# Whole-tile transfers and two wide rooms instead of half-tile transfers and four narrow ones, in a two-branch attention layer on one core

## The chip, the cores and the metric

The kernel runs on one core of a Trainium2 chip. Its engines are TensorE (PE, with its weight load PEld), VectorE (DVE), ScalarE (ACT), GpSimd (POOL) and SyncE (SP), which issues all transfers. The metric is the device time of one execution in microseconds, as the median of several runs. Less is better.

## The reference

One layer of a hybrid encoder is computed for a prompt of 1024 rows and a sample of 32 rows with the same weights. The width is 1024, and there are 8 heads of 64 in branch A and 8 in branch B.

```python
u = rmsnorm(h, g_pre) @ w_in                 # (rows, 4096): qA kA vA gA qB kB vB gB
oA = band_attention(qA, kA, vA, bias)        # 64-row chunks, own and 8 previous ones, softmax
oB = stick_breaking(qB, kB, vB)              # strictly causal, products of sigmoids
y = concat(oA * silu(gA), oB * silu(gB)) @ w_out
h = h + rmsnorm(y, g_post)
h = h + sigmoid(h @ w_ple_gate) * (p @ w_ple)
```

The sample attends to 512 cached rows as well. Outputs are both results, and the keys and values of both branches. Everything is in 32-bit floats.

## The kernel before, in words

**Recording and order.** The kernel isn't written in the order in which it runs. Each call on an engine is recorded as an operation; `Recorder.order` then simulates the engines with a table of costs and gives each operation a due time, and for each engine the operation with the earliest due time that is ready goes next. In the last pass each due time is shifted by ten times a number from two tables at the head of the file: `AHEAD_OF`, by engine and by the first letters of the written tile's name, and `AHEAD_AT`, by stage as well. `Recorder.emit` writes the instructions in the order so found. On the chip each engine takes its own list in order, and the engines wait for each other by semaphores. All recorded instructions carry the line of one helper, L793, so groups are told apart by the names of tiles.

**Stages.** Stage 0 loads and normalises x, turns it (hnh, hnl), and multiplies the first three column tiles; the per-layer product of the first four row tiles (`Ple(True)`, tiles `pleo`) fills TensorE meanwhile. Stages 1 to 8 weave attention of one head pair (tiles S, be, wTh, wTl, PV) with the projection by the next column tiles (`mm_kA` and so on). Stage 8 ends with the gate columns gA and gB. Stage 9 makes the rest of the per-layer product (`Ple(False)`, row tiles 4 to 8, tiles `ple`), stages 10 and 11 the output projection (`o0P` to `o3P`), stages 12 and 13 the product with w_ple_gate (`g0P` to `g3P`). Every 32-bit factor is split into a high part and a rest in a format that TensorE multiplies fast, and three products are added up.

**Column weights.** A column tile is 1024 x 128 of w_in. `load_w(j)` fetches it ahead of time, as two halves of 512 rows, each into a room of tag `wr` (names `wr_kA` and so on). `ensure(j)` casts each half to its high part (`wh`, on ScalarE; on GpSimd for the first three tiles) and subtracts for the rest (`wl`, on GpSimd). The 32 column tiles so make 64 transfers of 256 KB.

**The tag `wr`.** It has four rooms of 544 columns in 32-bit words on 128 partitions, given out in the order of the program. Besides raw weights it holds, at other times: the sample's split keys (`Kh`, `Kl`), its split cached values and weights (`Vh`, `Vl`, `wh`, `wl`), the late per-layer weights (`wpr`), the late per-layer products on their way to DRAM (`ple`, ten halves of a row tile; two of them take tag `bias` instead), the rows of x for the residual (`Row.load`, two halves per row tile), and product and residual of a gate (`Gate`, `pl` and `hh`). A room is taken again when the last reader of what it held is done; for a stored tile that is when its store has landed.

**Transfers.** SP issues all transfers of the program in the order that the planner found. A transfer whose room or data isn't ready holds up those behind it.

Of the kernel before, what the change touches and what calls it, by code (L numbers as in the profile page):

```python
# [8 lines left out]
F32 = mybir.dt.float32  # L9
F32R = mybir.dt.float32r  # L10
# [3 lines left out]
P = 128  # L14
# [6 lines left out]
KD = 8  # L21
# [6 lines left out]
AHEAD_OF = {  # L28
    ('ACT', 'Kh'): 847, ('ACT', 'L'): -810, ('ACT', 'Qfs'): 1255, ('ACT', 'be'): 110,
    ('ACT', 'gT'): 1212, ('ACT', 'kd'): 494, ('ACT', 'news'): -2591, ('ACT', 'om'): 22,  # L30
    ('ACT', 'stq'): 422, ('ACT', 'stv'): 214, ('ACT', 'v'): 132, ('ACT', 'w'): 1508, ('ACT', 'x'): -702,
    ('DVE', 'Kl'): -1025, ('DVE', 'Vh'): 168, ('DVE', 'Vl'): 157, ('DVE', 'diags'): -1166,
    ('DVE', 'news'): 142, ('DVE', 'o'): -939, ('DVE', 'oT'): -2081, ('DVE', 'sq'): -898,
    ('DVE', 'w'): 331, ('DVE', 'wTl'): -26, ('DVE', 'wl'): -2838, ('PE', 'PV'): -5, ('PE', 'PVl'): 51,
    ('PE', 'S'): -3, ('PE', 'Ss'): 12, ('PE', 'mm'): 7, ('PE', 'o'): -848, ('PE', 'ptws'): -36,
    ('PE', 'ptx'): -23, ('POOL', 'bias'): 574, ('POOL', 'kl'): -1392, ('POOL', 'o'): -923,
# [4 lines left out]
}  # L41
AHEAD_AT = {
# [3 lines left out]
    (1, 'SP', 'swap'): 1043, (2, 'ACT', 'kd'): -796, (2, 'ACT', 'om'): 57, (2, 'ACT', 'stq'): 426,  # L46
    (2, 'ACT', 'stv'): -553, (2, 'ACT', 'wh'): -314, (2, 'DVE', 'vx'): -235, (2, 'PE', 'PVl'): -89,
    (2, 'PE', 'mm'): 25, (2, 'PE', 'ptw'): -3, (2, 'POOL', 'o'): 176, (2, 'SP', 'wr'): -421,
    (3, 'ACT', 'stv'): -962, (3, 'ACT', 'whs'): -1728, (3, 'DVE', 'v'): -2339, (3, 'PE', 'PV'): 36,
# [19 lines left out]
}  # L69
# [729 lines left out]
def stream_step(  # L799
# [75 lines left out]
    def load_w(j):  # L875

        if j >= len(order) or j in raws:
            return
        kind, p = order[j]
        c0 = NAMES.index(kind) * 512 + p * P  # L880
        raws[j] = []
        for kh in range(2):
            raw = wpool.tile([P, 4, P], F32, tag="wr", name=f"wr_{kind}{p}_{kh}", bufs=4)
            dma(raw, w_in[0, kh * 512:(kh + 1) * 512, c0:c0 + P].rearrange("(k p) c -> p k c", p=P))
            raws[j].append(raw)

# [487 lines left out]
    def sample_attention(ab, gi):  # L1374
# [22 lines left out]
        def queries():  # L1397
# [11 lines left out]
            for a in range(2):  # L1409
                hi, lo = (wpool.tile([P, NK], F32R, tag="wr", name=f"K{x}{a}{nm}", bufs=4) for x in "hl")  # L1410
                pt = bx["Kc"][:, a, :]
                nc.vector.transpose(pt, pt)
                nc.scalar.copy(hi[:, 0:PAST], pt)
                nc.vector.tensor_tensor(lo[:, 0:PAST], pt, f(hi[:, 0:PAST]), ALU.subtract)
                new = ksS[:, at_[a], :]
                nc.scalar.copy(hi[:, PAST:NK], new)
                nc.vector.tensor_tensor(lo[:, PAST:NK], new, f(hi[:, PAST:NK]), ALU.subtract)
                Kh.append(hi)
                Kl.append(lo)
# [40 lines left out]
        def weights():  # L1460
            w1 = bx["w1"]
            def place(x, shape):
                return wpool.tile(shape, F32R, tag="wr", name=x + nm, bufs=4)

            def cached(b):
                pair = [place(f"V{x}{b}", [P, 2, 256]) for x in "hl"]
                nc.vector.tensor_copy(pair[0], bx["Vc"][:, b:b + 2, :])
                nc.vector.tensor_tensor(pair[1], bx["Vc"][:, b:b + 2, :], f(pair[0]), ALU.subtract)
                return pair

            old = [cached(0)]
            wh, wl = place("wh", [P, 4, P]), place("wl", [P, 4, P])
            pt = psum("T", f"ptw{nm}")
# [39 lines left out]
    class Ple:  # L1513
# [8 lines left out]
        def load_w(self, k, q):  # L1522
            name = f"wpr{k}_{q}{self.early}"
            if not self.early:
                raw = wpool.tile([P, 512], F32, tag="wr", name=name, bufs=4)
            elif (k, q) == (1, 1):
# [68 lines left out]
        def pieces(self, t, q):  # L1595
            t0, n = rows_of(t)
            hl = self.hl[t // 2]
            if self.early:
                if q == 0:
                    self.outs.append(at.tile([P, D], F32, tag=("kd1", "kl1", "L1", "v21")[t], name=f"pleo{t}"))  # L1600
                out = self.outs[t][:, HALF[q]]
            else:
                out = wpool.tile([P, 512], F32, tag="wr", name=f"ple{t}_{q}", bufs=4) if (t, q) not in ((5, 1), (6, 1)) else at2.tile([P, 512], F32, tag="bias", name=f"ple{t}_{q}", bufs=2)
            acc = psum(("S", "PV")[t - 2] if t > 1 and self.early else "mm" if self.early else "S", f"ple{t}_{q}")
# [9 lines left out]
            else:  # L1614
                nc.scalar.copy(out[0:n], acc[n:2 * n])
                nc.vector.tensor_tensor(out[0:n], acc[0:n], out[0:n], ALU.add)
            if not self.early or q:
                store = dma if not self.early else self.later.append
                args = (ple_dr[t0:t0 + n, HALF[q]], out[0:n]) if not self.early else ((ple_early[:, t, :], self.outs[t]),)
                store(*args)  # L1620

        later, outs = [], []

# [394 lines left out]
    class Row:  # L2018
# [7 lines left out]
        def load(self):  # L2026
            self.x = [wpool.tile([P, 512], F32, tag="wr", name=f"x2_{self.t}_{q}", bufs=4) for q in range(2)]
            for q in range(2):
                dma(self.x[q][0:self.n], x_prompt[0, self.t0:self.t0 + self.n, HALF[q]] if self.t < 8 else x_sample[0][:, HALF[q]])

# [24 lines left out]
    class Gate:  # L2055
        def __init__(self, t, cols, early=False):
# [6 lines left out]
            else:  # L2063
                self.pl = wpool.tile([P, 512], F32, tag="wr", name=f"pl{t}_{cols.start}", bufs=4)
                self.h = wpool.tile([P, 512], F32, tag="wr", name=f"hh{t}_{cols.start}", bufs=4)
            dma(self.pl[0:n], ple_early[32 * t:32 * t + 32].rearrange("q b c -> (q b) c")[:, cols] if t < 4 else ple_dr[self.rows, cols])
# [240 lines left out]
```

## Time and profile before

| | |
|---|---|
| median of 3 runs | 761.14 us (760.43 to 761.95) |
| the profiled execution | 760.99 us, span 759.1 us |
| PE busy | 750.3 us, 99% of the span, 4378 matmuls |
| PEld busy | 689.2 us, 91% |
| DVE, ACT, POOL busy | 606.5, 534.0, 447.5 us |
| transfers' queue | 168.63 MB, 75.9% of 16 engines' span |
| granted clock of TensorE | 1.000 |

The span runs from the first to the last instruction of one profiled execution. A busy PE is one that has a matmul under way, with ends that are modelled; its waits are listed apart. A transfer has an issue on SP and a landing, some microseconds later.

### The profile page before, as it was taken

The numbers are of one execution on the slowest core, as the hardware profiler recorded it, in microseconds if no ns is written. First come the engines' busy times: TensorE is split into PE (matmuls) and PEld (weight loads), VectorE is DVE, ScalarE is ACT, GpSimd is POOL, SyncE is SP. The second block draws the span as 40 slices with busy tenths as digits, with TensorE's granted clock in tenths as the row PEclk, the third lists the DMA queues.
The fourth block names the chain that finished last, engine by engine and source line by source line (L and its number), as shares of the span: only waits on it lengthen the run. The fifth ranks groups of instructions, "written<-read, shape, count | busy, mean of one in ns | idle before, by whom it ended". The sixth has DMA issues, their size and how long they took to land.

```text
span 759.1 us, 13838 instructions
## 1 busy us (share of the span) xinstructions
PE 750.3 (99%) x4378; PEld 689.2 (91%) x4378; DVE 606.5 (80%) x981; ACT 534.0 (70%) x1107; POOL 447.5 (59%) x496
## 2 busy tenths in 40 slices
PE   8999999999999999999999999999999999999997
PEld 7999999999999999999899999999998877888786
DVE  7827867899899998977899788867556788968975
ACT  6647874988687868976879786644348968874561
POOL 5724547773374653657774347877543449696553
PEclk9999999999999999999999999999999999999999
DMA  9645977868777758878878888996789956776864
GB/s 308 201 146 139 249 210 231 240 180 241 205 211 203 208 175 226 219 219 261 231 224 229 206 208 229 264 246 195 214 264 329 288 163 217 277 236 186 303 211 140
DMA packets 198971, 169.52 MB, mean 223 GB/s; under 512 B 66145, under 2 KB 158281, under 8 KB 198898
## 3 DMA queue, kind: packets, MB, share of 16 engines
q1 hardware_dynamic: 198898, 168.63, 75.9%
q8 instruction: 35, 0.57, 0.3%
q14 instruction: 38, 0.31, 0.1%
HBM read 107.82 MB, written 61.01 MB: 222 GB/s over the span
## 4 chain that ended last, share of the span: by engine, by line
PE 94%; DMA 2%; DVE 2%; ACT 1%; SPq 1%; issue 0%; ACTq 0%
PE mm_gB L793 6%; PE mm_kA L793 6%; PE mm_vB L793 6%; PE mm_gA L793 6%; PE mm_qB L793 6%; PE mm_vA L793 6%; PE mm_qA L793 5%; PE mm_kB L793 5%; PE SB L793 4%; PE PVB L793 4%; PE PVA L793 4%; PE SA L793 3%; PE ple L793 3%; PE g1P L793 3%; PE o3P L793 3%; PE o1P L793 3%
## 5 line engine op out<-in xcount | busy, mean ns | idle before, releaser
L793 POOL TENSOR_TENSOR be<-be 128x512 f32<-128x512 f32 (+8 forms) x66 | 86.1, 1313 | 56.5 <-ACT be L793 19.6
L793 DVE TENSOR_TENSOR_SCAN be<-be,unit 128x383 f32<-128x383 f32 (+7 forms) x100 | 93.2, 948 | 17.3 <-ACT be L793 16.2
L793 ACT ACTIVATE be<-SB 128x512 f32<-128x512 f32 (+5 forms) x192 | 83.8, 514 | 17.3 <-PE SB L793 12.6
L793 DVE TENSOR_TENSOR wTl<-be,wTh 128x640 fp32r<-128x640 f32 (+3 forms) x56 | 66.9, 1203 | 5.6 <-ACT wTh L793 5.5
L793 DVE STREAM_TRANSPOSE be<-be 128x640 f32<-128x640 f32 (+3 forms) x64 | 54.4, 849 | 6.7 <-POOL be L793 3.2
L793 ACT ACTIVATE be<-be,statA 128x640 f32<-128x640 f32 (+2 forms) x64 | 44.6, 698 | 15.3 <-DVE statA L793 11.5
L793 ACT CAST wTh<-be 128x640 fp32r<-128x640 f32 (+3 forms) x56 | 42.3, 762 | 1.8 <-DMA be<-swapB 1.6
L793 POOL TENSOR_TENSOR gB<-gB,gB 128x256 f32<-128x256 f32 x32 | 25.5, 820 | 20.2 <-DMA gB<-in_w_ple_gate_dram 20.2
L793 DVE CUSTOM_DVE_ANT_0 be<-SA,biasA 128x320 f32<-128x320 f32 (+2 forms) x64 | 30.0, 478 | 7.6 <-PE SA L793 4.0
L793 POOL TENSOR_TENSOR oB<-oB,oB 128x256 f32<-128x256 f32 x32 | 27.4, 875 | 9.9 <-DMA oB<-in_w_out_dram 9.8
L793 PE MATMUL SB<-kdB,LB 128*128 128x384 f32 (+5 forms) x96 | 33.1, 346 | 0.0
L793 PE MATMUL SB<-kl,LB 128*128 128x384 f32 (+5 forms) x96 | 33.1, 345 | 0.0
L793 PE MATMUL SA<-kdA,LA 128*128 128x320 f32 (+2 forms) x96 | 30.9, 326 | 0.6 <-DVE statA L793 0.6
L793 PE MATMUL SA<-kl,LA 128*128 128x320 f32 (+2 forms) x96 | 29.8, 314 | 0.0
L793 POOL TENSOR_TENSOR kl<-stkA,kdA 64x1024 fp32r<-64x1024 f32 (+2 forms) x9 | 19.7, 2189 | 15.2 <-ACT kdA L793 12.3
L793 POOL TENSOR_TENSOR oggB<-sggB,oggB 128x352 f32<-128x352 f32 x12 | 13.4, 1115 | 22.1 <-DVE sggB L793 22.0
L793 PE MATMUL PVB<-wTh,v2B 128*128 128x512 f32 (+2 forms) x96 | 25.4, 344 | 0.7 <-DVE v2B L793 0.7
L793 DVE TENSOR_TENSOR wTl<-ptwB,wTh 128x512 fp32r<-128x512 f32 (+3 forms) x40 | 20.1, 515 | 6.1 <-ACT wTh L793 6.0
L793 POOL TENSOR_TENSOR kl<-stkB,kdB 64x1024 fp32r<-64x1024 f32 x8 | 19.4, 2421 | 9.2 <-ACT kdB L793 7.6
L793 DVE TENSOR_TENSOR wTl<-ptwA,wTh 128x128 fp32r<-128x128 f32 (+3 forms) x48 | 22.1, 479 | 3.0 <-ACT wTh L793 2.8
L793 POOL TENSOR_TENSOR h<-h,x 128x512 f32<-128x512 f32 (+1 forms) x18 | 24.4, 1369 | 0.1
L793 ACT CAST wTh<-ptwB 128x512 fp32r<-128x512 f32 (+3 forms) x40 | 18.5, 480 | 8.2 <-PE PVB L793 4.6
(686 smaller groups left out, 2637.0 us busy)
## 6 DMA issues: line engine op xcount, KB each, us to landing
swapA<-be SPq DMA_DIRECT2D x24, 320.0 KB, 3.6
be<-swapA SPq DMA_DIRECT2D x96, 80.0 KB, 2.9
oB<-in_w_out_dram SPq DMA_DIRECT2D x16, 256.0 KB, 4.2
sum_dro<-oB SPq DMA_DIRECT2D x16, 256.0 KB, 3.0
gB<-in_w_ple_gate_dram SPq DMA_DIRECT2D x16, 256.0 KB, 4.1
sum_drg<-gB SPq DMA_DIRECT2D x16, 256.0 KB, 2.8
x<-in_x_prompt_dram SPq DMA_DIRECT2D x16, 256.0 KB, 3.4
h_dr<-h SPq DMA_DIRECT2D x8, 512.0 KB, 4.4
```

The costliest lines, as they stand in the source:

```text
L793: getattr(getattr(tc.nc, o.what[0]), o.what[1])(*args, **kw)
```

## The change

Raw weights of a column tile come in one transfer of 512 KB into a room of 1088 columns, and the two halves are views of it. The tag `wr` has two rooms of 1088 columns instead of four of 544, the same memory; what was two tiles of it is one tile with two parts (keys, cached values and weights of the sample, product and residual of a gate). The late per-layer weights are loaded in rows of 1024 columns (2 transfers instead of 4), the rows of x for the residual likewise (9 instead of 18), and the late per-layer product is stored by whole row tiles (5 instead of 10), all of them now through tag `wr`. The tables of shifts are replaced throughout; in the new ones no entry is for a stage after 8. What is multiplied, added and moved in bytes stays.

```diff
 AHEAD_OF = {
-    ('ACT', 'Kh'): 847, ('ACT', 'L'): -810, ('ACT', 'Qfs'): 1255, ('ACT', 'be'): 110,
...
+    ('ACT', 'L'): 382, ('ACT', 'Qfs'): 277, ('ACT', 'be'): -55, ('ACT', 'kd'): 1430, ('ACT', 'om'): 39,
...
 AHEAD_AT = {
-    (0, 'DVE', 'R'): 744, (0, 'DVE', 'sq'): 2099, (0, 'PE', 'ptx'): -63, (0, 'POOL', 'kl'): -512,
...
+    (0, 'ACT', 'hnh'): 2514, (0, 'PE', 'gpre'): -3844, (0, 'PE', 'mm'): -775, (0, 'PE', 'ple'): -493,
...
@@ load_w
-        raws[j] = []
-        for kh in range(2):
-            raw = wpool.tile([P, 4, P], F32, tag="wr", name=f"wr_{kind}{p}_{kh}", bufs=4)
-            dma(raw, w_in[0, kh * 512:(kh + 1) * 512, c0:c0 + P].rearrange("(k p) c -> p k c", p=P))
-            raws[j].append(raw)
+        raw = wpool.tile([P, KD, P], F32, tag="wr", name=f"wr_{kind}{p}", bufs=2)
+        dma(raw, w_in[0, :, c0:c0 + P].rearrange("(k p) c -> p k c", p=P))
+        raws[j] = [raw[:, 0:4], raw[:, 4:8]]
@@ sample_attention, queries
-                hi, lo = (wpool.tile([P, NK], F32R, tag="wr", name=f"K{x}{a}{nm}", bufs=4) for x in "hl")
+                both = wpool.tile([P, 2, NK], F32R, tag="wr", name=f"K{a}{nm}", bufs=2)
+                hi, lo = both[:, 0], both[:, 1]
@@ sample_attention, weights
-                return wpool.tile(shape, F32R, tag="wr", name=x + nm, bufs=4)
+                both = wpool.tile([P, 2] + shape, F32R, tag="wr", name=x + nm, bufs=2)
+                return both[:, 0], both[:, 1]
...
@@ Ple.load_w
-                raw = wpool.tile([P, 512], F32, tag="wr", name=name, bufs=4)
+                if q == 0:
+                    raw = wpool.tile([P, D], F32, tag="wr", name=name, bufs=2)
+                    dma(raw, w_ple[0, k * P:(k + 1) * P, :])
+                    self.raws[k, 0], self.raws[k, 1] = raw[:, L], raw[:, R]
+                return
@@ Ple.pieces
-                out = wpool.tile([P, 512], F32, tag="wr", name=f"ple{t}_{q}", bufs=4) if (t, q) not in ((5, 1), (6, 1)) else at2.tile([P, 512], F32, tag="bias", name=f"ple{t}_{q}", bufs=2)
+                if q == 0:
+                    self.outs[t] = wpool.tile([P, D], F32, tag="wr", name=f"ple{t}", bufs=2)
+                out = self.outs[t][:, HALF[q]]
...
-            if not self.early or q:
-                store = dma if not self.early else self.later.append
-                args = (ple_dr[t0:t0 + n, HALF[q]], out[0:n]) if not self.early else ((ple_early[:, t, :], self.outs[t]),)
-                store(*args)
+            if q:
+                if self.early:
+                    self.later.append((ple_early[:, t, :], self.outs[t]))
+                else:
+                    dma(ple_dr[t0:t0 + n], self.outs[t][0:n])
@@ Row.load
-            self.x = [wpool.tile([P, 512], F32, tag="wr", name=f"x2_{self.t}_{q}", bufs=4) for q in range(2)]
-            for q in range(2):
-                dma(self.x[q][0:self.n], x_prompt[0, self.t0:self.t0 + self.n, HALF[q]] if self.t < 8 else x_sample[0][:, HALF[q]])
+            x = wpool.tile([P, D], F32, tag="wr", name=f"x2_{self.t}", bufs=2)
+            dma(x[0:self.n], x_prompt[0, self.t0:self.t0 + self.n] if self.t < 8 else x_sample[0])
+            self.x = [x[:, c] for c in HALF]
@@ Gate.__init__
-                self.pl = wpool.tile([P, 512], F32, tag="wr", name=f"pl{t}_{cols.start}", bufs=4)
-                self.h = wpool.tile([P, 512], F32, tag="wr", name=f"hh{t}_{cols.start}", bufs=4)
+                both = wpool.tile([P, 2, 512], F32, tag="wr", name=f"pl{t}_{cols.start}", bufs=2)
+                self.pl, self.h = both[:, 0], both[:, 1]
```

More of the change, by code (lines that the diff above doesn't have):

```diff
@@ L28 @@
 AHEAD_OF = {
-    ('ACT', 'Kh'): 847, ('ACT', 'L'): -810, ('ACT', 'Qfs'): 1255, ('ACT', 'be'): 110,
[L30 to L34, printed above, removed]
@@ L35 @@
-    ('PE', 'S'): -3, ('PE', 'Ss'): 12, ('PE', 'mm'): 7, ('PE', 'o'): -848, ('PE', 'ptws'): -36,
-    ('PE', 'ptx'): -23, ('POOL', 'bias'): 574, ('POOL', 'kl'): -1392, ('POOL', 'o'): -923,
[4 rows of a table removed]
+    ('ACT', 'L'): 382, ('ACT', 'Qfs'): 277, ('ACT', 'be'): -55, ('ACT', 'kd'): 1430, ('ACT', 'om'): 39,
+    ('ACT', 'ot'): -3088, ('ACT', 'sgg'): 753, ('ACT', 'stv'): -1977, ('ACT', 'vt'): -1452,
+    ('ACT', 'wTh'): 75, ('ACT', 'wh'): -666, ('DVE', 'K'): 1032, ('DVE', 'L'): 305, ('DVE', 'V'): 773,
+    ('DVE', 'om'): -286, ('DVE', 'ot'): 361, ('DVE', 'over'): 253, ('DVE', 'sq'): 480,
@@ L41 @@
+    ('DVE', 'stats'): -2100, ('DVE', 'vx'): -322, ('DVE', 'w'): -208, ('DVE', 'wTl'): 179,
+    ('PE', 'S'): -5, ('PE', 'Ss'): 119, ('PE', 'ptw'): 12, ('PE', 'ptx'): -461, ('PE', 'ptxs'): 103,
+    ('POOL', 'be'): -869, ('POOL', 'ogg'): 330, ('POOL', 'om'): 949, ('POOL', 'w'): 1047,
[3 rows of a table added]
 }
 AHEAD_AT = {
[3 rows of a table removed]
-    (1, 'SP', 'swap'): 1043, (2, 'ACT', 'kd'): -796, (2, 'ACT', 'om'): 57, (2, 'ACT', 'stq'): 426,
-    (2, 'ACT', 'stv'): -553, (2, 'ACT', 'wh'): -314, (2, 'DVE', 'vx'): -235, (2, 'PE', 'PVl'): -89,
@@ L48 @@
-    (2, 'PE', 'mm'): 25, (2, 'PE', 'ptw'): -3, (2, 'POOL', 'o'): 176, (2, 'SP', 'wr'): -421,
-    (3, 'ACT', 'stv'): -962, (3, 'ACT', 'whs'): -1728, (3, 'DVE', 'v'): -2339, (3, 'PE', 'PV'): 36,
[19 rows of a table removed]
[8 rows of a table added]
+    (3, 'ACT', 'K'): -3754, (3, 'ACT', 'om'): -838, (3, 'DVE', 'Kcs'): 1619, (3, 'DVE', 'L'): -1338,
[4 rows of a table added]
+    (4, 'ACT', 'kd'): -868, (4, 'DVE', 'news'): 2426, (4, 'DVE', 'om'): -655, (4, 'DVE', 'w'): -521,
[7 rows of a table added]
+    (6, 'SP', 'swap'): -1593, (7, 'ACT', 'be'): 209, (7, 'ACT', 'v'): 809, (7, 'ACT', 'wTh'): 113,
+    (7, 'ACT', 'wh'): -1270, (7, 'DVE', 'V'): -2659, (7, 'DVE', 'kt'): -1461, (7, 'DVE', 'stats'): 1764,
[3 rows of a table added]
@@ L69 @@
+    (8, 'ACT', 'be'): 456, (8, 'ACT', 'sgg'): -406, (8, 'DVE', 'om'): -434, (8, 'DVE', 'sgg'): 1674,
+    (8, 'PE', 'PV'): -46, (8, 'PE', 'PVl'): -71, (8, 'PE', 'PVs'): -625, (8, 'PE', 'S'): 110,
+    (8, 'PE', 'Ss'): 209, (8, 'PE', 'mm'): 155, (8, 'PE', 'ptw'): -69, (8, 'PE', 'ptxs'): -1169,
+    (8, 'POOL', 'om'): -232, (8, 'POOL', 'over'): 807, (8, 'POOL', 'w'): -273, (8, 'SP', 'Kcs'): -446,
+    (8, 'SP', 'be'): 407, (8, 'SP', 'ogg'): -1002,
 }
@@ L1462, in place @@
             def place(x, shape):
-                return wpool.tile(shape, F32R, tag="wr", name=x + nm, bufs=4)
+                both = wpool.tile([P, 2] + shape, F32R, tag="wr", name=x + nm, bufs=2)
+                return both[:, 0], both[:, 1]
             def cached(b):
-                pair = [place(f"V{x}{b}", [P, 2, 256]) for x in "hl"]
+                pair = place(f"V{b}", [2, 256])
                 nc.vector.tensor_copy(pair[0], bx["Vc"][:, b:b + 2, :])
@@ L1471, in weights @@
             old = [cached(0)]
-            wh, wl = place("wh", [P, 4, P]), place("wl", [P, 4, P])
+            wh, wl = place("w", [4, P])
             pt = psum("T", f"ptw{nm}")
@@ L1599, in pieces @@
                 if q == 0:
-                    self.outs.append(at.tile([P, D], F32, tag=("kd1", "kl1", "L1", "v21")[t], name=f"pleo{t}"))
+                    self.outs[t] = at.tile([P, D], F32, tag=("kd1", "kl1", "L1", "v21")[t], name=f"pleo{t}")
                 out = self.outs[t][:, HALF[q]]
             else:
-                out = wpool.tile([P, 512], F32, tag="wr", name=f"ple{t}_{q}", bufs=4) if (t, q) not in ((5, 1), (6, 1)) else at2.tile([P, 512], F32, tag="bias", name=f"ple{t}_{q}", bufs=2)
+                if q == 0:
+                    self.outs[t] = wpool.tile([P, D], F32, tag="wr", name=f"ple{t}", bufs=2)
+                out = self.outs[t][:, HALF[q]]
             acc = psum(("S", "PV")[t - 2] if t > 1 and self.early else "mm" if self.early else "S", f"ple{t}_{q}")
@@ L1616, in pieces @@
                 nc.vector.tensor_tensor(out[0:n], acc[0:n], out[0:n], ALU.add)
-            if not self.early or q:
-                store = dma if not self.early else self.later.append
-                args = (ple_dr[t0:t0 + n, HALF[q]], out[0:n]) if not self.early else ((ple_early[:, t, :], self.outs[t]),)
-                store(*args)
-        later, outs = [], []
+            if q:
[3 more added lines that the diff above has]
+                    dma(ple_dr[t0:t0 + n], self.outs[t][0:n])
+        later, outs = [], {}
     pairs = [("A", 0), ("B", 0), ("A", 1), ("B", 1), ("A", 2), ("B", 2), ("A", 3), ("B", 3)]
```

49 rows, old and new, of tables (AHEAD_AT, AHEAD_OF) are left out of this document.

## The prediction

> **What bounds the kernel now.** I read the page first: the busy line, then the chain that ended last. After each engine's name stand its busy time, its share of the span and its instructions.
>
> ```profile
> span 759.1 us, 13838 instructions
> PE 750.3 (99%) x4378; PEld 689.2 (91%) x4378; DVE 606.5 (80%) x981; ACT 534.0 (70%) x1107; POOL 447.5 (59%) x496
> ...
> PEclk9999999999999999999999999999999999999999
> ...
> PE 94%; DMA 2%; DVE 2%; ACT 1%; SPq 1%; issue 0%; ACTq 0%
> ```
>
> TensorE issues almost without a break, at full clock, and 94% of the chain is its own work. A transfer, on the other hand, is on the chain for 2% and the queue that issues transfers (SPq) for 1%, some 7.6 us. So the question is how much time TensorE loses at all, and where. Second, the busy table by stretches (length, then PE, PEld, DVE, ACT, POOL, clock, DMA share, GB/s), third the waits of PE (total, times, longest), fourth the two ends of the chain.
>
> ```profile
> 0.00:540.00 540.00, 536.14 (x3383) 512.59 (x3384) 443.85 (x740) 397.03 (x832) 320.23 (x377) 1.00 0.78 218
> 540.00:584.00 44.00, 44.00 (x249) 41.03 (x249) 24.12 (x35) 23.18 (x46) 19.49 (x17) 1.00 0.84 271
> 584.00:754.00 170.00, 170.00 (x748) 135.62 (x746) 136.55 (x203) 113.24 (x229) 107.08 (x103) 1.00 0.71 232
> ```
>
> ```profile
> PE idle L793 <- DVE zeros L793: 1.2, 1, 1.2
> PE ple L793 <- ACT wph1True L793: 0.7, 1, 0.7
> PE PVB L793 <- DVE v2B L793: 0.7, 1, 0.7
> PE SA L793 <- DVE statA L793: 0.6, 1, 0.6
> PE PVA L793 <- DVE wTl L793: 0.2, 1, 0.2
> PE gpre L793 <- DVE wTl L793: 0.2, 1, 0.2
> PE PVA L793 <- ACT be L793: 0.2, 1, 0.2
> ```
>
> ```profile
> 3.34 6.68 DMA wpr_0True<-in_w_ple_dram
> ...
> 10.05 0.63 ACT wph1True L793
> ...
> 10.72 1.45 PE ple L793 x5
> ```
>
> ```profile
> 754.21 0.77 DVE uu L793 x2
> ...
> 755.79 0.42 DVE uu L793
> ```
>
> From 540 to 754 us PE is busy for all of 214.00 us: nothing can be won there, only lost. Before 540 it is idle for 540 - 536.14 = 3.9 us. The waits are 1.2 + 0.7 + 0.7 + 0.6 + 3 x 0.2 = 3.8 us, of which the first (1.2) is the unavoidable start; so 2.6 us are recoverable waits: 0.9 in the first 11 us (ple, gpre) and 1.7 in the attention stages. The tail behind the last matmul, 759.1 - 754.2 = 4.9 us, is vector work and the last store; its gate takes its rooms from other tags than the one changed. The head, up to 10.7 us, waits for the second half of the early per-layer weights, which the change leaves in halves.
>
> **The change part by part.**
>
> *Fewer issues.* Removed are 32 of 64 column-weight transfers, 9 of 18 loads of x for the residual, 2 of 4 late loads of the per-layer weights, 5 of 10 stores of the per-layer product: 48. On SP (nanoseconds min/median/max):
>
> ```profile
> L793 SPq DMA_DIRECT2D wr_kB<-in_w_in_dram x8: 367/396/995, 23.4 to 350.6; - x8
> L793 SPq DMA_DIRECT2D ple_dr<-ple x10: 319/387/845, 574.8 to 590.4; - x10
> ```
>
> With 0.39 us for each of the 48, SP is relieved of 18.7 us in 759. Almost all of that lies in time in which nobody on the chain waits for SP. Spread evenly it would take 18.7/759 = 2.5% off the 7.6 us of SPq on the chain, 0.2 us. But there is one place where a removable issue stands right on the chain. These are the chain between 276 and 310 us, and two rows of SP's order of time there:
>
> ```profile
> 280.50 0.72 SPq L793
> ...
> 283.29 0.39 SPq L793
> ...
> 283.72 3.82 DMA be<-swapB
> ...
> 287.58 1.68 DVE be L793 x2
> ...
> 289.33 0.56 PE SA L793 x2
> ```
>
> ```profile
> 280.50 0.72 SPq L793 DMA_DIRECT2D wr_qB<-in_w_in_dram  x1
> ...
> 283.29 0.39 SPq L793 DMA_DIRECT2D wr_vB<-in_w_in_dram  x1
> ```
>
> The second half of wr_qB and the first of wr_vB stand ahead of the fifth piece of a turned weight block; that piece lands late, the scans behind it delay the minimum statA, and PE loses the 0.6 us of the wait above. One issue fewer there is worth 0.39 to 0.72 us. I take -0.5 us for this term, bounds 0 (the new order puts something else there) and -0.6 (the whole wait).
>
> *Longer transfers.* A half (256 KB) against neighbours of 512 KB, median us to landing:
>
> ```profile
> h_dr<-h SPq DMA_DIRECT2D x8, 512.0 KB, 4.4
> ...
> be<-in_x_prompt_dram SPq DMA_DIRECT2D x4, 512.0 KB, 5.5
> ...
> wr_kB<-in_w_in_dram SPq DMA_DIRECT2D x8, 256.0 KB, 3.3
> ```
>
> A whole tile lands 1.1 to 2.2 us later than one half, but one landing then does for two. The first half's split is what gets later. It is tightest in the first stage, where GpSimd splits:
>
> ```profile
> 15.53 0.61 POOL L793 CAST wh_kA<-wr_kA 128x512 fp32r<-128x512 f32 x1
> ...
> 18.43 0.61 POOL L793 CAST wh_kA<-wr_kA 128x512 fp32r<-128x512 f32 x1
> 19.12 1.30 POOL L793 TENSOR_TENSOR wl_kA<-wr_kA,wh_kA 128x512 fp32r<-128x512 f32 x1
> ...
> 23.13 0.49 PE L793 MATMUL mm_kA<-hnh,wl_kA 128*128 128x352 f32 x2
> ```
>
> If both halves are there only at 18.43, the cast, the difference, the second cast and the second difference run from 18.43 to 18.43 + 2 x (0.61 + 1.30) + about 0.2 = 22.5 us; PE first wants a difference at 23.13. Covered, with 0.6 us to spare; cost 0, and if the landing is another 2 us later, at most 1.4 us. In the later stages the second half's landing sets the end of the split before as after: 0. What hides it all is that PE has matmuls of attention and of the tile before in its queue; gone, a late whole tile would cost at most the 1.1 to 2.2 us of its landing.
>
> The Trainium skill ("DMA: Bandwidth & Descriptors", Anatomy of one DMA) states that a transfer's semaphore can fire only once its last byte is confirmed, so a merged transfer gives up the early start on its first half: a rule against this change, and the head's casts (15.53, then 18.43) fit it. By its fixed cost of about 2.0 us a transfer, 48 fewer would be an estimated 96 us of transfer time, but with 2.6 us of waits to win, no such sum can appear; the rows above decide.
>
> *Rooms.* Two rooms of 1088 columns hold what four of 544 held. K and V of the sample were written and read in pairs anyway, and so were a gate's product and residual: 0, or some tenths if a pair is freed only with its later half, hidden under 170.00 us of busy PE. The exception is the per-layer product (`Ple.pieces`). Before, ten half products went through four rooms and two of another tag; now five whole ones share two rooms, and a room is free only when its store has landed.
>
> ```profile
> 573.12 0.59 ACT L793 COPY ple<-ple 128x512 f32<-128x512 f32 x1 [0.81 <-PE ple L793]
> ...
> 578.32 0.58 ACT L793 COPY ple<-ple 128x512 f32<-128x512 f32 x1
> ```
>
> ```profile
> 575.00:580.00 5.00, 5.00 (x24) 4.14 (x23) 2.12 (x4) 3.93 (x9) 1.30 (x1) 1.00 1.06 356
> ...
> DMA to landing us min/median/max: 4.6/5.8/6.8
> ```
>
> The second line of the last fence is the landing time of these stores (the tile `ple`). Tile 4's two copies end at 573.1 + 0.6 and about 574.8; its store, issued at 574.9, lands at 580.7 (median) or 581.7, with the DMA engines full (share 1.06) perhaps 2 later. The fifth copy, tile 6's first, went at 578.32 and would go at 580.7 to 583.7: 2.4 to 5.4 us later. Meanwhile two to four finished products stay in PSUM. PE stops only if it wants a bank then. Bounds: 0 (banks free) and +5.4 us. I take +0.3: eight banks for at most four held products, and a planner that can draw these products forward into the gB stage; the likelier end is nearest the row of 44.00 busy us.
>
> *The order.* All tables of small shifts are replaced, so nearly every instruction finds another neighbour. Work on PE is the same 4378 matmuls. What a new order can win is the recoverable 2.6 us of waits, less the 0.5 counted above; what it can lose has no bound in PE's waits, and I take one from the other engines' (total, times, longest):
>
> ```profile
> POOL be L793 <- ACT be L793: 19.6, 10, 5.6
> ```
>
> I take -1.8 us: with 18.7 us less on SP the turned blocks come earlier, and I assume that the new order closes most of what is left; bounds -2.1 and +5.6.
>
> **Sum.** The profiled execution took 760.99 us (span 759.1 and 1.9 around it), 0.15 under the median of three, 761.14; the runs lie within 0.2%, so 0.2% (1.5 us) is about what can be told from no change. 760.99 - 0.5 + 0 + 0.3 - 1.8 = 759.0 us.
>
> **Rivals.**
> - *Nothing moves* (760 to 762): the removed issues were all hidden, and the new order has waits of its own of some 2 to 3 us. For it: 99% busy; against it: the issue on the chain at 280 us.
> - *The product's rooms stall PE* (slower). Place: between 578 and 590 us. The fifth copy on ACT waits for a store; ACT is in order, so the left-hand casts for the first output products queue behind it, and PE, busy in all 44.00 us before, stops. It decides once the held products and the new accumulators want a ninth bank. At the upper bound, 5.4 less the 1 to 2 us by which PE is ahead, 4 us: with half the winnings above 761 - 1 + 4 = 764. For it: the DMA share over 1 there; against it: the queue can be reordered.
> - *A worse order* (slower): waits in the attention stages, such as those ten of `be`, reach PE: 761 + 1.5 to 761 + 6, centre 764.5. Nothing in this profile excludes it, because only 3.9 us of PE's first 540 are idle.
> - *All waits go* (756 to 757.6): the whole 2.6 us and a head shortened by 1 to 2 us: 761 - 4 = 757. Against it: the head's halves are untouched.
>
> **Chances.** The forecast (757.6 to 759.5) 0.37; all waits gone 0.08; nothing moves 0.26; the product's rooms 0.12; a worse order 0.17. So faster 0.45, same 0.26, slower 0.29. The likeliest case's own range is 757.6 to 759.5; the range for 8 in 10 reaches into both sides, from 755.5 to 766.
>
> **What would show it.** Right: 48 transfers fewer on SP; PE waits under 1.5 us between 12 and 540 us; PE busy for all but some tenths between 540 and 754; the last matmul at about 752. The product's rooms: a wait of ACT's copies of `ple` on a transfer, and PE gaps near 580. Whole tiles too late: PE or POOL waiting for `wr` or `wl` of a column tile. What would make the prediction wrong: a new wait of several us in the attention stages that the old order did not have, or a shorter head, since the order of the first ten transfers is redrawn too.

## The result, and the profile after

The changed kernel is slower: its median is 765.01 us (763.10 to 767.92, six runs), that of the kernel before beside it 761.04 us (760.36 to 761.95, six runs). The ratio is 1.0054, 95% interval 1.0042 to 1.0065. Ratios take fast runs alone: a slow run of the kernel before, of 4225 us, beside three_moves, before_other, after_other and after_other2, is left out of theirs. The profiled execution of the changed kernel is the slowest of its six: 767.92 us, with a span of 766.1 us. So what its trace shows lost, 7.0 us of span, is more than the 4.0 us between the medians, and its rows say where rather than exactly how much.

The page of the changed kernel: the span, the busy line and the chain that ended last.

```profile
span 766.1 us, 13760 instructions
PE 754.8 (99%) x4378; PEld 690.6 (90%) x4378; DVE 610.8 (80%) x981; ACT 535.5 (70%) x1107; POOL 451.3 (59%) x496
...
PE 84%; DMA 6%; DVE 4%; ACT 3%; issue 1%; POOL 1%; SPq 1%; ACTq 0%; DVEq 0%; POOLq 0%
```

The matmuls are the same 4378, and PE is "99%" busy as before. That share hides the loss: busy time itself rose from 750.3 to 754.8 us. The clock doesn't explain it (1.000 and 0.999 granted, under 1 us). A likely reading is that small delays don't show as idle: the record of a projection matmul lasts 0.32 us (median) and the next matmul starts 0.16 us after it (median), so one that comes 0.1 us late leaves no gap. The chain is no measure of the loss either. PE held 94% of it before and holds 84% now, and transfers went from 2% to 6%; but of two kernels shown below, before_other (760.81 us) has 85% and before_fresh3 (766.01 us) has 94%:

```profile
PE 85%; DVE 5%; ACT 2%; DMA 2%; issue 2%; POOL 2%; SPq 0%; DVEq 0%; ACTq 0%; POOLq 0%
```

```profile
PE 94%; DVE 3%; ACT 1%; issue 1%; DMA 0%; SPq 0%; DVEq 0%; ACTq 0%
```

The busy table of the changed kernel by the stretches of the prediction (the last one reaches to 761 here, since the kernel ends later):

```profile
0.00:540.00 540.00, 533.49 (x3334) 507.27 (x3335) 440.57 (x734) 395.17 (x827) 318.93 (x373) 1.00 0.78 216
540.00:584.00 44.00, 44.00 (x268) 42.61 (x267) 27.16 (x38) 20.91 (x43) 24.66 (x20) 1.00 0.79 254
584.00:761.00 177.00, 177.00 (x779) 140.69 (x778) 140.87 (x207) 119.01 (x239) 106.44 (x104) 1.00 0.72 233
```

The count in brackets is the useful number. By 540 us PE had done 3383 matmuls before and has done 3334 now. It is 49 behind, and with 540/3383 = 0.16 us for each that is some 7.8 us: about all that was lost was lost by then. The first output product (o0P) says the same: it begins at 583.8 us before and at 590.9 us now, 7.1 us later. From 540 us on PE is busy without a gap, as before, and the tail, which in the chain begins at 761.31 us, is 4.8 us against 4.9. In the first 540 us idle time is 540 - 533.49 = 6.5 us against 3.9; those 2.6 us and the 4.5 us by which busy time rose make up the 7.0, but for rounding.

The waits of PE in the changed kernel (total, times, longest):

```profile
PE PVsB L796 <- ACT wsB L796: 1.5, 1, 1.5
PE idle L796 <- DVE zeros L796: 1.2, 1, 1.2
PE ptp L796 <- DMA pp<-in_p_prompt_dram: 1.0, 1, 1.0
PE SA L796 <- ACT stkB L796: 1.0, 1, 1.0
PE mm_gA L796 <- DVE sggA L796: 0.3, 1, 0.3
PE ptwA L796 <- DVE statA L796: 0.3, 1, 0.3
PE SB L796 <- DVE wTl L796: 0.3, 1, 0.3
```

None of the waits of the kernel before is in the list but the unavoidable start (1.2), and three new ones of 1.0 to 1.5 us stand in their place. Each can be followed to its cause. The first is in the head, where SP now issues a weight load ahead of the second part of pp. SP's order of time and the chain there:

```profile
1.54 0.35 SPq L796 DMA_DIRECT2D wpr_0True<-in_w_ple_dram  x1
1.93 0.43 SPq L796 DMA_DIRECT2D pp<-in_p_prompt_dram  x1
```

```profile
1.93 4.01 DMA pp<-in_p_prompt_dram
...
5.99 1.12 PE ptp L796 x4
```

The second is on ScalarE at 293 us: the copy stkB, which frees the bank that SA wants, stands behind casts of 1.05, 1.05 and 0.62 us.

```profile
293.10 1.05 ACT L796 CAST kdA<-stkA 64x1024 fp32r<-64x1024 f32 x1
294.18 1.05 ACT L796 CAST LA<-stqA 64x1024 fp32r<-64x1024 f32 x1
295.25 0.62 ACT L796 CAST wh_qB<-wr_qB 128x512 fp32r<-128x512 f32 x1
295.77 0.45 ACT L796 COPY stkB<-mm_kB 128x352 f32<-128x352 f32 x1
```

The third is on the chain at 525 us. The sample's weights wsB take the wide room that the raw column tile wr_gB leaves, and they have to wait until both its halves are split; those splits stand on ScalarE behind a cast (wTh) that waits for a transfer of a turned block:

```profile
518.16 5.99 DMA be<-swapB
...
525.07 0.63 ACT wh_gB L796
...
527.27 1.28 POOL wl_gB L796
...
528.58 0.59 ACT wsB L796
```

Further ahead on the same chain stands the landing of a whole column tile, wr_gA, for 7.16 us from 499.33 us on. It is the only one of `wr` on the chain; in narrow_rooms, where the transfers are halves again, the chain has one of wr_gB for 6.41 us from 510.41 us on.

Transfers of the tag `wr` in the changed kernel, KB each and median us to landing (before, the halves of the weights took 3.3 to 4.9 in the same view; the eight kinds of whole tiles take 4.7 to 6.9):

```profile
wr_kA<-in_w_in_dram SPq DMA_DIRECT2D x4, 512.0 KB, 6.9
...
wr_kB<-in_w_in_dram SPq DMA_DIRECT2D x4, 512.0 KB, 4.7
...
ple_dr<-ple SPq DMA_DIRECT2D x4, 512.0 KB, 5.9
```

The change makes three kinds of difference at once, and each is a theory of the 4 us: WHOLE (a transfer of a whole tile lands too late), ROOMS (two wide rooms come free too late) and ORDER (the new order is a worse one, whatever the transfers and rooms). The experiments take them apart.

### The profile page after: what moved, and what is told of

It reads as the page before. It is cut to its first block, busy times and chain, and to the rows that moved or that the text cites. A ratio compares the mean times of both kernels' runs of the same rounds, so it can differ in the third digit from the quotient of the medians.

```text
span 766.1 us, 13760 instructions
## 1 busy us (share of the span) xinstructions
PE 754.8 (99%) x4378; PEld 690.6 (90%) x4378; DVE 610.8 (80%) x981; ACT 535.5 (70%) x1107; POOL 451.3 (59%) x496
## 4 chain that ended last, share of the span: by engine, by line
PE 84%; DMA 6%; DVE 4%; ACT 3%; issue 1%; POOL 1%; SPq 1%; ACTq 0%; DVEq 0%; POOLq 0%
PE mm_kA L796 6%; PE mm_qA L796 6%; PE mm_qB L796 6%; PE mm_gB L796 5%; PE mm_vA L796 5%; PE mm_vB L796 5%; PE mm_kB L796 4%; PE SB L796 4%; PE PVB L796 3%; PE PVA L796 3%; PE ple L796 3%; PE SA L796 3%; PE g1P L796 3%; PE o3P L796 3%; PE o1P L796 3%; PE g0P L796 3%
## 5 line engine op out<-in xcount | busy, mean ns | idle before, releaser
L796 POOL TENSOR_TENSOR be<-be 128x128 f32<-128x128 f32 (+8 forms) x66 | 83.4, 1271 | 59.8 <-ACT be L796 21.8
L796 ACT ACTIVATE be<-SB 128x384 f32<-128x384 f32 (+5 forms) x192 | 83.5, 504 | 15.0 <-PE SB L796 8.3
L796 ACT ACTIVATE be<-be,statA 128x640 f32<-128x640 f32 (+3 forms) x64 | 44.6, 697 | 13.7 <-DVE statA L796 11.2
L796 DVE CUSTOM_DVE_ANT_0 be<-SA,biasA 128x320 f32<-128x320 f32 (+4 forms) x64 | 29.7, 480 | 4.1 <-PE SA L796 3.9
L796 PE MATMUL PVB<-wTl,v2B 128*64 128x128 f32 (+2 forms) x96 | 25.6, 359 | 0.0
L796 PE MATMUL ptwA<-ident,be 128*128 128x128 f32 x120 | 24.9, 274 | 0.3 <-DVE statA L796 0.3
L796 PE MATMUL ptwB<-ident,be 128*128 128x128 f32 x112 | 24.4, 272 | 0.2 <-POOL be L796 0.2
```

Of the source, the lines that this page charges most:

```text
L796: getattr(getattr(tc.nc, o.what[0]), o.what[1])(*args, **kw)
```

## The experiments

Each kernel is compared with runs of the kernel before beside it on the same chip, five chips in all; the medians of the kernel before were 760.75 to 761.53 us there. So rows are best compared by their ratios. All numbers are in one table; the names are explained below it.

| kernel | transfers, rooms | order | median us | ratio to before, 95% |
|---|---|---|---|---|
| changed | whole, 2 | its tables | 765.01 | 1.0054 (1.0042 to 1.0065) |
| halves_again | halves, 2 | that of the changed kernel | 764.12 | 1.0044 (1.0032 to 1.0056) |
| narrow_rooms | halves, 4 | that of the changed kernel | 764.65 | 1.0048 (1.0036 to 1.0060) |
| before_no_shifts | halves, 4 | empty tables | 764.93 | 1.0058 (1.0045 to 1.0071) |
| after_no_shifts | whole, 2 | empty tables | 763.87 | 1.0048 (1.0033 to 1.0063) |
| three_moves | whole, 2 | changed, 5 instructions moved | 764.42 | 1.0034 (1.0021 to 1.0047) |
| before_other | halves, 4 | near that of before | 760.81 | 0.9992 (0.9983 to 1.0000) |
| before_other2 | halves, 4 | near that of before | 761.14 | 1.0006 (0.9997 to 1.0015) |
| after_other | whole, 2 | near that of changed | 765.46 | 1.0049 (1.0033 to 1.0065) |
| after_other2 | whole, 2 | near that of changed | 765.92 | 1.0056 (1.0043 to 1.0070) |
| before_fresh1 to 4 | halves, 4 | searched anew | 762.12, 764.64, 766.01, 764.27 | 1.0015, 1.0049, 1.0058, 1.0044 |
| after_fresh1 to 4 | whole, 2 | searched anew | 763.11, 765.89, 769.09, 762.98 | 1.0031, 1.0064, 1.0099, 1.0029 |

**The old transfers, then the old rooms, in the new order.** The order of the changed kernel was kept to the instruction, and only what the transfers and rooms are was put back. In halves_again each of the 48 whole transfers is issued as two halves, one right behind the other, into the same wide room:

```diff
-        dma(raw, w_in[0, :, c0:c0 + P].rearrange("(k p) c -> p k c", p=P))
+        two(halves_k, raw, w_in[0, :, c0:c0 + P].rearrange("(k p) c -> p k c", p=P))
```

narrow_rooms has the halves as well, and each wide room is two rooms of 544 columns again, each of them free when its own half is done:

```diff
     def take(self):
+        if self.tag == "wr":
+            n = int(self.room.split(".")[1])
...
+            self.real = Twin(*(... tag=f"wr.{2 * n + k}" ... for k in range(2)))
+            return
```

> The changed kernel with its order of instructions on every engine frozen, but each of its 48 whole transfers issued as two halves, one right behind the other, into the same wide room. Theory ORDER (the loss sits in the order that the new tables of shifts draw; neither transfers nor rooms matter by themselves): 765 us, at most 1 us more for 48 issues of 0.4 us. Theory ROOMS (a wide room is free only when its later half has been read; that costs the 4 us): also 765, since the rooms stay wide. Theory WHOLE (a whole transfer lands 1 to 2 us later than its first half did and what waits for the first half is late): 762 to 763 if the halves' landings count, though a reader that waits for both tells nothing.

> The same frozen order, with halves as transfers and four rooms of 544 columns instead of two of 1088: each half is a tile of its own, so a half is taken again when its own readers are done. This is the kernel before with the order of the changed one. ORDER: 764 to 766 us, as the changed kernel. ROOMS: 761 to 762. In the trace the wait of ScalarE's wsB for GpSimd's wl_gB (1.66 us) and TensorE's wait for wsB (1.5 us) should go under ROOMS and under ORDER alike; they differ in what this is worth in the end: 1.5 us at most under ORDER, 3 to 4 us under ROOMS.

Measured: 764.12 and 764.65 us. With the old transfers and the old rooms, but the new order, the kernel is as slow as the changed one. So the 48 transfers are worth nothing that can be told, and neither are the rooms; the intervals of the ratios leave room for 2 us at most. PE's waits in narrow_rooms (of over 0.4 us) show the same places as in the changed kernel:

```profile
PE ptp L816 <- DMA pp<-in_p_prompt_dram: 2.1, 1, 2.1
PE idle L816 <- DVE zeros L816: 1.2, 1, 1.2
PE SA L816 <- ACT stkB L816: 0.7, 1, 0.7
```

ORDER holds; WHOLE (762 to 763) and ROOMS (761 to 762) fall as causes of the 4 us in this order. The long wait for wsB isn't in narrow_rooms (0.4 us are left), and not in halves_again either, which has the wide rooms:

```profile
PE ptp L796 <- DMA pp<-in_p_prompt_dram: 1.2, 1, 1.2
PE idle L796 <- DVE zeros L796: 1.2, 1, 1.2
PE SA L796 <- ACT stkB L796: 0.7, 1, 0.7
```

So it isn't the rooms alone that make it, and without it the total is hardly better. What a frozen order can't show is whether whole tiles force the planner into worse orders; the next experiments ask that.

**Both kernels without tables.** With both tables empty the planner orders by due times alone.

```diff
-AHEAD_OF = { ... }
-AHEAD_AT = { ... }
+AHEAD_OF = {}
+AHEAD_AT = {}
```

> The kernel before with both tables of shifts empty, so that the order follows from due times alone. ORDER: clearly slower than before, by 4 us or more (765 to 775), because the shifts are what makes the order good. ROOMS and WHOLE say nothing on it alone.

> The changed kernel with both tables empty. ORDER: within 2 us of the kernel before without shifts, either side. ROOMS: 3 to 4 us slower than that. A gain of the 48 saved issues that only shows where no table hides it: 2 us or more faster than that.

Measured: 764.93 us for the kernel before and 763.87 us for the changed one. On level terms the change is not slower by anything that can be told (ratios 1.0058 and 1.0048, with intervals that overlap). The old tables are worth 764.93 - 760.78 = 4.2 us on the chip; the new ones nothing that shows (763.87 without, 765.01 with them). By these two runs the whole difference between the two kernels is what the old tables won.

**Taking away the three largest waits.** In the changed kernel's finished order five instructions are moved ahead of others on the same engine (engine, number of the instruction, number of the one that it is to precede):

```diff
+MOVES = (('SP', 3, 2), ('ACT', 402, 400), ('ACT', 732, 731), ('ACT', 733, 731), ('ACT', 734, 731), )
...
-        return out
+        return self.moved(out)
```

> The changed kernel with its finished order kept but for five instructions, moved at the three places where TensorE waits longest in its trace: on SP the second load of pp goes ahead of the first load of w_ple (wait of ptp 1.0 us); on ScalarE the copy stkB<-mm_kB of stage 5 goes ahead of the cast to LA (wait of SA 1.0 us); on ScalarE the two casts of wr_gB and the sigmoid between them go ahead of the cast wTh<-be that waits for a transfer (wait of PVsB 1.5 us). PLACES (the loss sits in these three waits, and nothing takes their place): 765.0 - 3.5 = about 761.5 us, and the three rows are gone from TensorE's waits. SPREAD (the loss is spread over many small gaps, and a wait that is taken away comes back later): 764 to 765 us; the rows are gone, but the gaps between matmuls add up to as much as before.

Measured: 764.42 us, which is 0.6 us below the changed kernel; by the two ratios to the kernel before (1.0034 and 1.0054, with intervals that overlap) it is 1.5 us. It is not 3.5, and the kernel is still 2.6 us slower than the kernel before (1.0034), so PLACES falls: the loss doesn't sit in these three waits alone. The 3.5 us have to be read with care, though. They are those of the slowest execution of the changed kernel; halves_again, with the same order and a profiled execution of 764.83 us, shows 1.2 us for pp, 0.7 for stkB and none for wsB, 1.9 us together. PE's waits in three_moves:

```profile
PE SA L830 <- DVE statA L830: 1.2, 1, 1.2
PE idle L830 <- DVE zeros L830: 1.2, 1, 1.2
PE ptx L830 <- DVE be L830: 0.7, 1, 0.7
PE ple L830 <- POOL wpl0True L830: 0.6, 1, 0.6
...
PE ptp L830 <- DMA pp<-in_p_prompt_dram: 0.3, 1, 0.3
```

The rows for stkB and wsB are gone and that for pp fell from 1.0 to 0.3. At two of the three places the next late thing stands there instead: in the head the split of a weight (0.6, at 10.0 us) and the tile be (0.7, at 13.4 us), and SA at 296.6 us now waits 1.2 us for statA, where it waited 1.0 us for stkB at 296.3. That is SPREAD, as far as these two places go. A wait in the list names what happened to come last, and what is won by its removal is the distance to the next one.

**Other orders in the same structure.** Is the old order a good one because halves and narrow rooms allow it, or by chance? Two random walks from each kernel's tables, through tables whose order the planner rates equal or better, give neighbours of each order: the PE stream keeps its sequence but for 20 to 155 of 4378 matmuls.

```diff
 AHEAD_OF = {
-    ('ACT', 'Kh'): 847, ('ACT', 'L'): -810, ('ACT', 'Qfs'): 1255, ('ACT', 'be'): 110,
+    ('ACT', 'S'): -1400, ('ACT', 'be'): 110, ('ACT', 'gT'): 1212, ('ACT', 'h'): -52,
...
```

> The kernel before (halves, four rooms) with other numbers in its two tables: a random walk through tables whose order the planner itself rates as good as that of the kernel before. About 50 of 864 SP issues and 155 of 4378 matmuls stand elsewhere. CHANCE (an order that the planner rates equal comes out anywhere in 760 to 766 us on the chip, and that of the kernel before is one that came out well): 762.5 to 766 us. STRUCTURE (halves and four rooms let an order run as the planner means it): 760 to 762 us.

> The kernel before with tables from a second walk near its own, in which only steps were kept that the planner rates no worse; it rates the result 0.4 us better, and 20 of 4378 matmuls stand elsewhere. If the planner's rating holds on the chip near an order that does well (the version that would beat both kernels): 760.4 to 760.8 us. CHANCE also for small changes: 760 to 763 us.

> The changed kernel (whole transfers, two wide rooms) with other numbers in its two tables, from a random walk through tables whose order the planner rates as good. CHANCE: anywhere from 760.5 to 766 us, and not like the changed kernel's 765.0 in particular. STRUCTURE (whole rooms let no order run as the planner means it): 763.5 to 766 us.

> As after_other, from a second walk that took only tables that the planner rates at least as good as the last. CHANCE: anywhere from 760.5 to 766 us, and another value than that of after_other. STRUCTURE: 763.5 to 766 us.

Measured: 760.81 and 761.14 us near the old order, 765.46 and 765.92 us near the new one. That is what STRUCTURE foretold; the 760.4 to 760.8 us that the planner's rating promised for before_other2 did not come. It does not decide, though, because neighbours inherit the order that they come from: after_other has the wait of SA on stkB again, as long as in the changed kernel.

```profile
PE ptp L848 <- DMA pp<-in_p_prompt_dram: 1.4, 1, 1.4
PE idle L848 <- DVE zeros L848: 1.2, 1, 1.2
PE SA L848 <- ACT stkB L848: 1.0, 1, 1.0
```

So tables were searched anew from empty ones, four times in each structure, by the same steps. These orders are much farther off: in before_fresh1 some 690 of 4378 matmuls stand elsewhere than in the kernel before. The edit is again the two tables.

> The kernel before (halves, four rooms) with tables that were searched anew from empty ones, by small random steps that are kept when the planner rates the new order no worse. The planner rates the four orders of this call within 1 us of each other (mean of the two on halves 0.1 us above that of the two on whole tiles). Some 690 of 4378 matmuls stand elsewhere than in the kernel before. STRUCTURE (under halves and four rooms an order keeps on the chip what it wins in the plan, under whole tiles and two rooms it does not): 761 to 763 us, and 3 us or more below the two on whole tiles. CHANCE (what an order is worth on the chip scatters by some us, in either structure): 761 to 767 us, with no gap between the two pairs.

> As before_fresh1, from another seed; the planner rates it 1.0 us worse than that. STRUCTURE: 762 to 764 us. CHANCE: 761 to 767 us.

> As before_fresh1 (halves, four rooms, tables searched anew from empty ones), third seed; the planner rates it as good as that. CHANCE (orders scatter by some us in either structure, with the same middle): 761 to 766 us. SMALL STRUCTURE (the scatter is there, but whole tiles and two rooms move its middle up by 1 us or more): under 763 us.

> As before_fresh3, fourth seed; rated 0.5 us better. CHANCE: 761 to 766 us. SMALL STRUCTURE: under 763 us.

> The changed kernel (whole transfers, two wide rooms) with tables searched anew from empty ones in the same way; the planner rates it 0.3 us better than before_fresh2 and 0.7 us worse than before_fresh1. STRUCTURE: 765 to 768 us. CHANCE: 761 to 767 us, as likely below as above the two on halves.

> As after_fresh1, from another seed; the planner rates it as good as before_fresh1. STRUCTURE: 765 to 768 us. CHANCE: 761 to 767 us; under 762 us would show that whole tiles and two rooms allow an order as good as that of the kernel before.

> As after_fresh1 (whole transfers, two wide rooms, tables searched anew), third seed; rated 0.8 us worse than before_fresh3. CHANCE: 761 to 767 us. SMALL STRUCTURE: 764 us or more.

> As after_fresh3, fourth seed; rated 0.4 us worse than that. CHANCE: 761 to 767 us. SMALL STRUCTURE: 764 us or more.

Measured: 762.1 to 766.0 us on halves, 763.0 to 769.1 us on whole tiles. The mean ratios are 1.0042 and 1.0056, 1.1 us apart. The four values scatter with a standard deviation of 0.0019 and 0.0033, which makes the difference of the means 1.1 us with a standard error of about 1.4 us. STRUCTURE falls: two of the whole-tile orders beat three of the four on halves. CHANCE stands, but for its upper end: after_fresh3, with 769.1, is above the 767 that it gave. SMALL STRUCTURE, which was asked of the last four (halves under 763, whole tiles at 764 or more), has only after_fresh3 on its side. Nor does the planner's rating tell which order does well: before_fresh1 and before_fresh3 are rated alike and came out 3.9 us apart (by the ratios 3.3), and after_fresh4, rated last of all eight, came out second best. Each order has its own late places. PE's waits in before_fresh3 and in after_fresh4, three rows of each:

```profile
PE idle L856 <- DVE zeros L856: 3.3, 1, 3.3
PE SA L856 <- DVE statA L856: 2.9, 1, 2.9
PE PVA L856 <- DVE wTl L856: 0.3, 1, 0.3
```

```profile
PE idle L856 <- DVE zeros L856: 3.3, 1, 3.3
PE ptxsA L856 <- DVE wsA L856: 0.5, 1, 0.5
PE PVsB L856 <- DVE V2sB L856: 0.4, 1, 0.4
```

In the slower one a single wait for the statistic statA takes 2.9 us; in the faster one no wait after the start is over 0.5.

**What stays open.** A shift of the middle by whole tiles of some 1 us either way is neither shown nor excluded; four orders a side tell about 3 us. Why the old order runs so well on the chip, 1.1 us below the best of eight searched anew, isn't explained by any single row; how its tables were found isn't known here, and if they were picked by runs on the chip, it may simply be the best of many draws. The old order on wide rooms wasn't tried: it takes the two halves of two column tiles through one narrow room, one after the other, which a room for the whole tile doesn't permit. The old tables in the changed kernel weren't tried either. No version beats the kernel before by what can be measured: before_other, the lowest, has 0.9992 with an interval that ends at 1.0000, and its second walk gave 1.0006.

## Why the prediction was wrong

The forecast was 759.0 us; 765.0 came, inside the range for 8 in 10 but on the other side. The rival that happened is *a worse order* (762.5 to 767, centre 764.5), which had 0.17. Its number came closer than its mechanism: the waits of `be` that it named did grow on GpSimd (for ScalarE's `be` from 19.6 to 26.0 us), but of waits for `be` PE's list shows 0.2 us.

- *The order* is the step that failed: -1.8 us was taken, "I assume that the new order closes most of what is left". Measured, the new order alone is worth about +3.9 us (narrow_rooms, 764.65, against the kernel before beside it, 760.78), and +3.3 with the wide rooms (halves_again, 764.12). Of the 6.0 us between forecast and result this term is 5.1 to 5.7. The assumption took the old order for a typical one with 2.6 us still to win. It was an exceptional one: nine orders that don't come from it, eight searched anew and the changed kernel's own, run at 762.1 to 769.1. A change that redraws the order loses that first; and with PE busy for 99% there was little to win, which the prediction itself put at 2.6 us. The bound was named there (+5.6); the error was to take the value at the favourable end.
- *Fewer issues*, -0.5 us: not realised. The wait of SA on statA that it was to remove is gone from the list (the longest wait on statA that is left has 0.3 us), but a wait of SA on stkB of 1.0 us stands 7 us later in the same stage. With the order held, 48 issues more cost nothing that can be told: halves_again is no slower than the changed kernel.
- *Longer transfers*, 0: right within what can be told, though the landings were mis-sized. Whole tiles land 4.7 to 6.9 us after their issue against 3.3 to 4.9 of the halves, 0.3 to 3.1 us later by kind (1.1 to 2.2 were forecast). In the head, which was called the tightest place, the whole wr_kA took 9.0 us where each half had taken 9.3. Halves instead of wholes in the same order change the time by -0.9 us, with runs of the changed kernel that spread over 4.8 us.
- *Rooms*, +0.3: too small to be told (narrow_rooms and halves_again differ by 0.5 us the other way), and for the per-layer product nothing showed. Its five stores (four of 512 KB, one of 128 KB) land in 5.6 to 6.5 us, where the ten halves took 4.6 to 6.8; ScalarE's ten copies don't wait for one, and PE has no gap from 540 us on. The one wait of PE behind a wide room is another one, wsB at 528 us (1.5 us). The prediction had passed over it with "0, or some tenths", because before 540 us it looked at pairs that are written together, not at what takes the room next. In total it cost little: halves_again has no such wait and narrow_rooms 0.4 us of it, and they are 0.9 and 0.4 us below the changed kernel. It is read from the slowest execution, so the others may not have it.
- The sign that was to show it wrong, "a new wait of several us in the attention stages that the old order did not have", did not come as it was put: the longest new wait has 1.5 us. There are two new waits there, of 1.0 and 1.5 us, one of 1.0 us for pp in the head, and the 4.5 us by which busy time rose.
- The estimate from the Trainium skill ("DMA: Bandwidth & Descriptors", Anatomy of one DMA), 96 us of transfer time less, was rightly set aside: put back as halves in the same order, the 48 transfers cost nothing that can be told. That section gives its figure for transfers that GpSimd issues; here SP issues all of them. Its rule on the last byte fits the later landings (medians 4.7 to 6.9 us against 3.3 to 4.9), and they cost nothing that can be told either.

## What to carry to other kernels

When one engine is busy for 99% and the order of all others is planned by hand or by a search, a change that forces a new order may be first of all a new draw, as it was here: price it by how orders scatter (here 761 to 769 us for the same work), not by the waits that the old order still has. Test such a change with the order held fixed, and compare the structures with their tuning taken away on both sides, before any of the difference is put down to transfers or rooms. Removing the three longest waits brought back 0.6 to 1.5 us here, where the slowest execution's list had 3.5, so a list of waits is no list of winnings; and a list from one execution should be one whose time is near the median.

## What the runs showed that had not been expected

- The scatter within one program seems to differ: the kernel before spread over 1.3 us beside halves_again (760.31 to 761.57, eleven runs) and over 3.0 us beside after_fresh4 (760.12 to 763.16, seventeen runs), the changed one over 4.8 us (763.10 to 767.92, six), after_fresh4 over 6.1 us (761.23 to 767.28, twelve). It isn't the order alone: halves_again and narrow_rooms, in the changed kernel's order, spread over 2.3 and 2.5 us in five runs. What makes it is not shown.
- A store of the per-layer product of twice the size took no longer to land: a median of 5.9 us for 512 KB, of 6.3 us for 256 KB before. A weight tile of twice the size did: 4.7 us against 3.3 for wr_kB.
